# Retention's queries and keys computed with tokens on the partitions, in two blocks of 1024 columns

## The chip, the cores and the metric

One Trainium2 chip; the kernel runs on one of its cores. The metric is device microseconds from the start to the end of one execution, the median over several; lower is better. Four engines do the arithmetic: PE (TensorE, matrix multiply into PSUM), DVE (VectorE), ACT (ScalarE) and POOL (GpSimd, nearly unused here). SP (SyncE) issues most transfers. Each engine works through its own queue.

## The reference, cut to what matters

A decoder layer on 256 tokens of width 2048: a gated feed-forward half with its norm, two mixers side by side (retention and windowed attention), a second feed-forward half, and a gated embedding. All of it is float32. The change concerns how retention's queries and keys come out of the normalised stream `h`:

```python
rq, rk, rv, rg, aq, ak, av, gate_r, gate_a = jnp.split(h @ w_in[i], SPLIT_POINTS, axis=-1)
rq = rotary(rq.reshape(B, S, RET_HEADS, RET_DK), positions, RET_DK, RET_THETA)
rk = rotary(rk.reshape(B, S, RET_HEADS, RET_DK), positions, RET_DK, RET_THETA) * (RET_DK ** -0.5)
...
def rotary(x, pos, n_rot, theta):
    ...
    cos = jnp.cos(ang)[:, :, None, :]; sin = jnp.sin(ang)[:, :, None, :]
    x1, x2 = xr[..., :half], xr[..., half:]
    rot = jnp.concatenate([x1 * cos - x2 * sin, x2 * cos + x1 * sin], axis=-1)
```

Queries and keys are 1024 columns each (8 heads of 128); the product runs over 2048 rows of weights.

## The kernel before, in words

**Float32 by splitting.** Each float32 operand is split into a high part (a cast to the type `float32r`, on ACT) and a low part (operand minus high part, on DVE). A product is the sum of three matmuls: low by high, high by high, high by low. `ht` holds the normalised stream turned, with features on the partitions: for each of 16 blocks of 128 features, 256 tokens of the high part and 256 of the low part side by side.

**Two layouts of a product.** With *features on the partitions* (`features_out`, `features_chunk`, lines 461 and 469) the weights are the stationary operand: a high block meets all 512 columns of `ht` (high and low tokens at once), a low block only the 256 high ones. The result has features on the partitions; its two halves of 256 columns have to be added (`joined`, lines 1287 and 1288). With *tokens on the partitions* (`tokens_chunk`, `Sum.add`, lines 510 to 512) `ht` is the stationary operand and 512 columns of weights move, three matmuls a product.

**Chunks.** Weights come in chunks of 512 KB, a tile of 128 x 1024 float32. A `Single` unit is one chunk: one load, one cast on ACT (line 162) and one subtraction on DVE (line 164). In features layout a chunk takes 8 matmuls of 512 columns and 8 of 256, in tokens layout 12 of 512.

**Seven products for eight.** `block` computes two neighbouring groups of 512 columns with tokens on the partitions. A unit "P" is a pair of Singles (24 matmuls). A unit "S" (`Seven`) is one 2 x 2 step of Strassen's method in Winograd's form: 7 products, so 21 matmuls. It needs sums of the weights (`Seven.make`, lines 277 to 298: four passes on ACT, eight on DVE) and *forms* of the stationary operand (`forms_sums`, lines 588 to 591; `forms_split`), and at the end a common part (`seven_common`, lines 634 to 639) and four additions (lines 1669 to 1672).

**The order of the work.** Every engine's order is the program's. A planner emits it: `take` hands out the next unit that is made, and after its matmuls `done` frees its slots and calls `fill`, which makes units (the split) while less than 45 units of time lie ready, and loads further ones while less than 90 do. A Single counts 12, a Seven 21. `slots_for_weights(n)` says how many of the 46 slots of 4 KB per partition the planner may hold: a Single holds 1 loaded and 2 made, a Seven 2 loaded, 8 while it is made, 7 made. All other 4 KB tiles (sums, forms, rotated tables, results) take theirs from the same 46. PSUM has 8 banks, one per 512 columns of float32.

After each unit `run_side` runs one job of each of three lists: `side` (jobs in order), `slow` and `lazy` (generators that go on by one step). On `lazy` lies `sums_ahead`: in spare time it computes weight sums for the second feed-forward half and writes them to memory (lines 372 to 386).

**The stages around the change**, in `mixers`:
- *rv, first two column groups* (tokens layout, 16 Singles). The first six run while the norm before still turns its last rows (`norm.first`); the other ten run plainly, from about 713 us of the profile on, under `slots_for_weights(24)`. `values` then splits the four sums out of PSUM (lines 113 and 114).
- *rqk* (features layout): 8 groups of 256 columns, 4 chunks each, 32 in all, under `slots_for_weights(14)`. After each group `joined` writes a half tile. The generator `angles` on `slow` builds the table of cosines and sines (`rotary_table`, lines 993 to 1020) and then turns the groups (`turn_by_angle`, lines 1293 to 1297: a shuffle within the partitions and three passes).
- *rv, last two groups* (16 Singles), *rg* (retention's gate, 32 Singles) with retention itself on `side`, and then attention, the two mixing gates and the output projections. The gates `ga0` and `ga1` (1143 to 1226 us) and `mr0` and `mr1` (1269 to 1354 us) use Seven units. The forms of `ht` that the gates need are computed in the stage before them.

`Turn` turns a tile by a transfer: `part` separates the 16-bit words (two copies on ACT), `move` is a transposing DMA on SP's queue, `join` puts the words together (two copies on ACT).

Of the kernel before, what the change touches and what calls it, by code (L numbers as in the profile page):

```python
# [8 lines left out]
F32 = mybir.dt.float32  # L9
# [61 lines left out]
def layer(ctx: ExitStack, tc: tile.TileContext, io):  # L71
# [16 lines left out]
    def slot(shape, dt, name):  # L88
        return slots.tile(shape, dt, tag="slot", name=name)
# [1216 lines left out]
    RET_UNITS = [units_of(order, SEVEN[: order.count("S")]) for order in ("SPSPSPSP", "PSPSPPPP")]  # L1306
    gate_keys = lambda b: lambda n, p: ("w_in_f2", 29 + 4 * b + 2 * n, p)
# [33 lines left out]
    def mixers(ht, norm, residual, keepers, away):  # L1341
        rhs = lambda k: (ht[:, k, :S], ht[:, k, S:])
        both_halves = lambda k: ht[:, k, :]
        rq = [slot([P, 4, S], F32, f"rq{j}") for j in range(2)]
        rk = [slot([P, 4, S], F32, f"rk{j}") for j in range(2)]

        def rotated(grp, ps):
            who = (rq, rk)[grp // 4][grp % 4 // 2]
            to = who[:, grp % 2 * 2 : grp % 2 * 2 + 2, :]
            joined(ps, f"rr{grp}", to)  # L1350
            unturned[grp] = to

        unturned = {}

        def rotations():
            for grp in (0, 4, 1, 5, 2, 6, 3, 7):
                while grp not in unturned:
                    yield
                to = unturned.pop(grp)
                turn_by_angle(to, f"rr{grp}", to, *trig["r"], SH_R)  # L1360
                yield
                yield
# [29 lines left out]
        def angles():  # L1392
            yield from rotary_table("r")
            yield from rotations()
            yield from rotary_table("a")

        slow.append(angles())
# [240 lines left out]
        made = {}  # L1638
        forms = lambda p: made[p // 2](p % 2)
# [3 lines left out]
        for j in range(4):  # L1643
            def before(c, j=j):
                if j < 2:
                    return
                g = j - 2
                if c == 0:
                    sums = forms_sums(whole([ht[:, 4 * g : 4 * g + 4, :]], f"gaf{g}w"))
                    keep["f", g] = sums  # L1650
                if c == 1:
                    hi, lo = (slot([P, 8, P], F32R, f"gaf{g}{w}") for w in "hl")
                    made[g] = forms_split(keep.pop(("f", g)), hi, lo)
# [7 lines left out]

        def mixer_block(name, units, keys, lhs):

            ps = [banks(name + w) for w in "ab"]
            got = []
            block(name, units, keys, lhs, forms, block_sums(ps, units, KD), lambda *a: got.extend(seven_common(*a)))
            weave_all()
            e, w, z = got
            dve.tensor_tensor(e[:, 0], e[:, 0], ps[0][0], ALU.add)
            dve.tensor_tensor(e[:, 1], w[:, 1], ps[1][0], ALU.add)  # L1670
            for t in range(2):
                dve.tensor_tensor(z[:, t], z[:, t], ps[t][1], ALU.add)
            return [e, z]
# [400 lines left out]
```

## Time and profile before

| | |
|---|---|
| median of 3 runs | 2226.69 us (2225.88 to 2227.86) |
| profiled execution | 2229.62 us, of which its span on the core 2227.6 us |
| granted TensorE clock | 0.999 |
| PE busy | 2215.5 us (99%) |
| DVE busy | 2011.8 us (90%) |
| ACT busy | 1451.7 us (65%) |
| rqk's matmuls | first at 740.2 us, last at 829.4 us |

Times in the views are microseconds from the start of the span. In a timeline row the first number is the start, the second the busy time, then engine, line, operation, output<-input and count; square brackets give the idle time of the engine before and what ended it. A row with a count above 1 merges neighbours; starts that lie closer together than the busy time mean that the engine overlaps successive instructions.

### The profile page before, as it was taken

Reading aid. Unit: us, or ns where it says so; the run is one execution under the profiler, and the core shown is the slowest. Engines: PE = TensorE matmul, PEld = TensorE weight load, DVE = VectorE, ACT = ScalarE, POOL = GpSimd, SP = SyncE. Lnnn points to the kernel's source line nnn. Section 1 sums busy time; section 2 is a strip of 40 time slices with the busy share of each in tenths; the row PEclk is TensorE's granted clock in tenths of the full one; section 3 lists DMA queues with packets and bytes.
Section 4 is the critical chain, followed back from the end, with each engine's and each line's share of the span. In section 5 each row is a group of like instructions: output and inputs, shape, how many; then the busy total and the mean of one; then the engine's idle time right before and its main releaser. Section 6 shows DMA issues by size and latency. Waiting matters only on the chain.

```text
span 2227.6 us, 29127 instructions
## 1 busy us (share of the span) xinstructions
PE 2215.5 (99%) x10116; PEld 1832.7 (82%) x10116; DVE 2011.8 (90%) x2656; ACT 1451.7 (65%) x1691; POOL 48.4 (2%) x62
## 2 busy tenths in 40 slices
PE   9999999999999999999999999999999999999998
PEld 7788888888888888888788888888888877888887
DVE  5999999999988889889999888779999999899887
ACT  5877777777565545557866567466767678665553
POOL 0000000000000000000000000000000000000000
PEclk9999999999999999999999999999999999999999
DMA  9979889977686889846976578888899898777771
GB/s 315 259 227 264 249 241 263 255 239 235 225 301 238 296 280 331 274 171 228 293 232 232 174 216 323 306 302 269 290 313 312 292 265 260 215 242 234 283 290 69
DMA packets 303339, 573.91 MB, mean 258 GB/s; under 512 B 98764, under 2 KB 103756, under 8 KB 303192
## 3 DMA queue, kind: packets, MB, share of 16 engines
q1 hardware_dynamic: 293576, 541.70, 72.5%
q0 software_dynamic: 7632, 27.79, 6.7%
q10 hardware_dynamic: 1984, 2.58, 0.4%
q8 instruction: 79, 1.29, 0.2%
q14 instruction: 68, 0.56, 0.1%
HBM read 490.20 MB, written 33.55 MB: 235 GB/s over the span
## 4 chain that ended last, share of the span: by engine, by line
PE 92%; DMA 3%; DVE 3%; issue 2%; ACT 1%; SPq 0%; ACTq 0%; POOLq 0%; DVEq 0%
PE rqk L461 3%; PE f1g L512 3%; PE f1g L510 3%; PE f1g L511 3%; PE f2g L510 2%; PE f2g L511 2%; PE f2g L512 2%; PE f1u L512 2%; PE f1u L510 2%; PE f1u L511 2%; PE f2u L512 2%; PE f2u L510 2%; PE f2u L511 2%; PE aqk L461 2%; PE f2d L512 1%
## 5 line engine op out<-in xcount | busy, mean ns | idle before, releaser
L164 DVE TENSOR_TENSOR lw_in_f<-rw_in_f,hw_in_f 128x1024 fp32r<-128x1024 f32 x132 | 158.2, 1219 | 14.5 <-ACT hw_in_f L162 14.3
L164 DVE TENSOR_TENSOR lf_gu<-rf_gu,hf_gu 128x1024 fp32r<-128x1024 f32 x123 | 145.1, 1219 | 22.8 <-ACT hf_gu L162 22.1
L162 ACT CAST hf_gu<-rf_gu 128x1024 fp32r<-128x1024 f32 x123 | 123.3, 1048 | 29.7 <-DMA rf_gu<-in_f_gu 27.8
L293 ACT CAST hvf_gu<-vf_gu 128x1024 fp32r<-128x1024 f32 x83 | 87.5, 1055 | 76.5 <-DVE vf_gu L289 62.6
L284 ACT CAST huf_gu<-uf_gu 128x1024 fp32r<-128x1024 f32 x83 | 87.3, 1052 | 76.6 <-DVE uf_gu L280 69.3
L162 ACT CAST hw_in_f<-rw_in_f 128x1024 fp32r<-128x1024 f32 x132 | 132.5, 1049 | 6.9 <-DMA rw_in_f<-in_w_in_f 4.2
L164 DVE TENSOR_TENSOR lf_down<-rf_down,hf_down 128x1024 fp32r<-128x1024 f32 x96 | 115.6, 1220 | 20.5 <-ACT hf_down L162 16.3
L162 ACT CAST hf_down<-rf_down 128x1024 fp32r<-128x1024 f32 x96 | 98.5, 1049 | 27.3 <-DMA rf_down<-in_f_down 11.8
L287 DVE TENSOR_TENSOR lf_gu<-rf_gu,hf_gu 128x1024 fp32r<-128x1024 f32 x83 | 101.1, 1218 | 0.0
L298 DVE TENSOR_TENSOR lvf_gu<-vf_gu,hvf_gu 128x1024 fp32r<-128x1024 f32 x83 | 101.1, 1218 | 0.0
L296 DVE TENSOR_TENSOR luf_gu<-uf_gu,huf_gu 128x1024 fp32r<-128x1024 f32 x83 | 101.1, 1218 | 0.0
L277 ACT CAST hf_gu<-rf_gu 128x1024 fp32r<-128x1024 f32 x83 | 86.8, 1046 | 8.4 <-DMA rf_gu<-in_f_gu 8.4
L512 PE MATMUL f1g<-lf_gu,xt 128*128 128x512 f32 x223 | 87.1, 391 | 1.1 <-DVE lf_gu L164 1.1
L510 PE MATMUL f1g<-hf_gu,xt 128*128 128x512 f32 x223 | 87.0, 390 | 0.1
L511 PE MATMUL f1g<-hf_gu,xt 128*128 128x512 f32 x223 | 86.8, 389 | 0.0
L510 PE MATMUL f2g<-hf_gu,ht 128*128 128x512 f32 x196 | 76.4, 390 | 0.0
L512 PE MATMUL f2g<-lf_gu,ht 128*128 128x512 f32 x196 | 76.3, 389 | 0.0
L511 PE MATMUL f2g<-hf_gu,ht 128*128 128x512 f32 x196 | 76.3, 389 | 0.0
L512 PE MATMUL f1u<-lf_gu,xt 128*128 128x512 f32 x180 | 70.1, 390 | 0.0
L510 PE MATMUL f1u<-hf_gu,xt 128*128 128x512 f32 x180 | 70.1, 390 | 0.0
L511 PE MATMUL f1u<-hf_gu,xt 128*128 128x512 f32 x180 | 70.0, 389 | 0.0
L182 POOL DMA_DIRECT2D lf_gu<-rf_gu x37 | 32.2, 871 | 1636.9 <-DMA rf_gu<-in_f_gu 1105.6
(1568 smaller groups left out, 7220.3 us busy)
## 6 DMA issues: line engine op xcount, KB each, us to landing
rf_gu<-in_f_gu SPq DMA_DIRECT2D x362, 512.0 KB
rf_down<-in_f_down SPq DMA_DIRECT2D x176, 512.0 KB
rw_in_f<-in_w_in_f SPq DMA_DIRECT2D x148, 512.0 KB
lf_gu<-rf_gu POOLq DMA_DIRECT2D x37, 512.0 KB, 8.5
rw_rv<-in_w_rv SPq DMA_DIRECT2D x32, 512.0 KB
rw_ret<-in_w_ret SPq DMA_DIRECT2D x32, 512.0 KB
rw_mix<-in_w_mix SPq DMA_DIRECT2D x32, 512.0 KB
rw_pg<-in_w_pg SPq DMA_DIRECT2D x32, 512.0 KB
```

The costliest lines, as they stand in the source:

```text
L162: act.copy(c.hi, c.raw)
L164: dve.tensor_tensor(c.lo, c.raw, c.hi, ALU.subtract)
L277: act.copy(a.hi, a.raw)
L284: act.copy(uh, u)
L287: dve.tensor_tensor(a.lo, a.raw, a.hi, ALU.subtract)
L293: act.copy(vh, v)
L296: dve.tensor_tensor(ul, u, uh, ALU.subtract)
L298: dve.tensor_tensor(vl, v, vh, ALU.subtract)
L461: pe.matmul(ps[f], hi[:, kk, f * P : (f + 1) * P], rhs(k), start=k == 0, stop=k == n_k - 1,)
L510: pe.matmul(o, al, bh, start=first, stop=False)
L511: pe.matmul(o, ah, bh, start=False, stop=False)
L512: pe.matmul(o, ah, bl, start=False, stop=self.left == 0)
```

## The change

The eight feature groups of rqk become two calls of `mixer_block`, one for the queries (1024 columns) and one for the keys, with tokens on the partitions. Each is six P units and two S units: 14 units of the planner in place of 16 chunks. The order is PPPSPSPP and PPSPSPPP.

- The forms of `ht` for the four S positions (pairs 0 to 3) are built in the rv stage, at its units p = 4 and 5 (`forms_step`). They are dropped after the keys and built again for the gates as before.
- `rotary_table("r")` moves from rqk into the ten plain units of rv. At the eleventh step, after the first unit of the queries, `wide_tables` turns cosine and sine with four transposes on PE into one PSUM bank and spreads them with four copies on ACT to two tiles of 128 x 2 x 512.
- Each block gives two result tiles with tokens on the partitions. `rotated` turns each by the angle (two crossed products of 512 columns with runs of 16, one product and one addition of 1024) and then by a transfer: `part`, `move`, `join`. The queries' 13 side jobs run beside the keys' units, the keys' beside the third group of rv.
- `joined`, the shuffles and `turn_by_angle` no longer run for retention. The table for attention (`rotary_table("a")`) starts when the keys are joined.
- `sums_ahead` runs 2 items with 3 units between steps and then 5 with 2, in place of 3 and 4 with 2.

```diff
+    QK_UNITS = [units_of(order, SEVEN[: order.count("S")]) for order in ("PPPSPSPP", "PPSPSPPP")]
+    qk_keys = lambda b: lambda n, p: ("w_in_f2", 4 * b + 2 * n, p)
...
-        for grp in range(8):
-            plan_features([("w_in_f", grp)], KD)
+        for b in range(2):
+            block_units(QK_UNITS[b], qk_keys(b))
...
+        def forms_step(g, step):
+            if step == 0:
+                sums_of[g] = forms_sums(whole([ht[:, 4 * g : 4 * g + 4, :]], f"gaf{g}w"))
+            else:
+                hi, lo = (slot([P, 8, P], F32R, f"gaf{g}{w}") for w in "hl")
+                made[g] = forms_split(sums_of.pop(g), hi, lo)
...
+        def wide_tables():
+            cos, sin = trig["r"]
+            ps = bank("rtab").rearrange("p (w t n) -> p w t n", w=2, t=2)
+            for j, v in enumerate((cos, sin)):
+                for t in range(2):
+                    pe.transpose(ps[:, j, t], v[:, t * P : t * P + P], ident)
+            for j, w in enumerate("cs"):
+                wide[w] = slot([P, 2, 512], F32, f"rtab{w}")
+                for t in range(2):
+                    act.copy(
+                        wide[w][:, t].rearrange("p (h n) -> p h n", h=4), ps[:, j, t][:, None, :].broadcast_to([P, 4, P])
+                    )
+
+        def rotated(v, name, to):
+            halves = lambda x: x.rearrange("p t (q two n) -> p two (t q) n", two=2, n=16)
+            crossed = {}
+            def cross():
+                x = crossed["x"] = slot([P, 2, 512], F32, name + "x")
+                for two in range(2):
+                    dve.tensor_tensor(
+                        halves(x)[:, two], halves(v)[:, 1 - two], halves(wide["s"])[:, two], ALU.mult
+                    )
+            def scale():
+                dve.tensor_tensor(v, v, wide["c"], ALU.mult)
+            def add():
+                dve.tensor_tensor(v, v, crossed.pop("x"), ALU.add)
+                crossed["t"] = Turn(v, name)
+            def join():
+                to.append(slot([P, 4, S], F32, name + "t"))
+                crossed.pop("t").join(to[-1])
+            return [
+                cross, scale, add, lambda: crossed["t"].part(), lambda: crossed["t"].move(), idle, join,
+            ]
...
         slots_for_weights(24)
+        def angles():
+            yield from rotary_table("r")
+            wide_tables()
+            yield
+            while len(rk) < 2:
+                yield
+            yield from rotary_table("a")
+        slow.append(angles())
         for p in range(FRONT_PAIRS, KD // 2):
             for n in range(2):
+                if p in (4, 5):
+                    forms_step(p - 4, n)
                 u = take(("w_rv", n, p))
...
         slots_for_weights(14)
-        lazy.append(sums_ahead(ahead[:3], 3, 2))
-        lazy.append(sums_ahead(ahead[3:7], 2, 2))
-        for grp in range(8):
-            ps = banks(f"rqk{grp}")
-            features_out([(("w_in_f", grp), ps)], KD, both_halves)
-            rotated(grp, ps)
+        lazy.append(sums_ahead(ahead[:2], 3, 3))
+        lazy.append(sums_ahead(ahead[2:7], 2, 2))
+        for b in range(2):
+            got = mixer_block("rqk"[0] + "qk"[b], QK_UNITS[b], qk_keys(b), rhs)
+            jobs = [rotated(v, f"r{'qk'[b]}{n}", (rq, rk)[b]) for n, v in enumerate(got)]
+            side.extend(jobs[0][:3] + [jobs[0][3], jobs[1][0], jobs[0][4], jobs[1][1], jobs[1][2], jobs[1][3], jobs[1][4], jobs[0][6], idle, jobs[1][6]])
+        made.clear()
```

`mixer_block` itself only moves up in the file, and `forms_step` takes over the two steps that the gates' stage had written out.

More of the change, by code (lines that the diff above doesn't have):

```diff
@@ L1343, in mixers @@
         both_halves = lambda k: ht[:, k, :]
[L1344 to L1362, printed above, removed]
+        rq, rk = [], []
@@ L1636, in mixers @@
             attention_features(grp)
-        made = {}
-        forms = lambda p: made[p // 2](p % 2)
         lazy.append(sums_ahead(ahead[7:10], 2, 2))
@@ L1646, in before @@
                     return
[L1647 to L1653, printed above, removed]
+                if c < 2:
+                    forms_step(j - 2, c)
             ps = banks(f"gt{j}")
@@ L1660, in mixers @@
         assert not side
[L1662 to L1673, printed above, removed]
         slots_for_weights(22)
```

22 lines of the change are left out of this document (17 added, 5 removed).

## The prediction

> **What bounds the kernel now.** I read the page first, then the busy times by stage, then rqk's own instructions, then DVE's queue around the start of rqk, because several parts of the change land there.
>
> ```profile
> span 2227.6 us, 29127 instructions
> PE 2215.5 (99%) x10116; PEld 1832.7 (82%) x10116; DVE 2011.8 (90%) x2656; ACT 1451.7 (65%) x1691; POOL 48.4 (2%) x62
> DVE  5999999999988889889999888779999999899887
> PE 92%; DMA 3%; DVE 3%; issue 2%; ACT 1%; SPq 0%; ACTq 0%; POOLq 0%; DVEq 0%
> 717.00:740.20 23.20, 23.20 (x104) 19.23 (x103) 13.66 (x13) 14.01 (x16) 0.00 (x0) 1.00 1.02 396
> 740.20:785.00 44.80, 44.80 (x258) 39.41 (x258) 39.40 (x60) 22.67 (x31) 0.00 (x0) 1.00 0.77 265
> 829.70:873.10 43.40, 43.40 (x193) 35.95 (x192) 42.74 (x63) 22.41 (x27) 0.00 (x0) 1.00 0.98 344
> 1143.40:1226.00 82.60, 82.60 (x370) 68.19 (x370) 80.88 (x98) 51.43 (x57) 0.00 (x0) 1.00 0.63 214
> ```
>
> PE carries the chain. In the stage rows (window, length, then busy time of PE, weight loads, DVE, ACT) PE is busy for the whole of each window, so a microsecond of matmuls removed is a microsecond gained, and a microsecond of idle PE is one lost. DVE is the second engine: 13.66 of 23.20 us before rqk, 39.40 of 44.80 in its first half, 42.74 of 43.40 just behind it. The gates' stage, with eight Seven units, runs at 80.88 of 82.60 and PE still isn't idle. So a full DVE is bearable as long as it works far enough ahead.
>
> **The matmuls.** First timeline and chain rows, then the group that shows PE's only wait in the blocks of this kind.
>
> ```profile
> 735.25 0.39 PE L512 MATMUL rv<-lw_rv,ht 128*128 128x512 f32 x1
> 737.29 0.39 PE L512 MATMUL rv<-lw_rv,ht 128*128 128x512 f32 x1
> 740.01 0.39 PE L512 MATMUL rv<-lw_rv,ht 128*128 128x512 f32 x1
> 740.24 1.98 PE L461 MATMUL rqk<-ht,hw_in_f 128*128 128x512 f32 x8
> 742.21 0.95 PE rqk L469 x8
> 743.16 1.84 PE rqk L461 x8
> L512 PE MATMUL mr1a<-lw_ret,rett 128*128 128x512 f32 x26 | 10.2, 393 | 0.5 <-DVE lw_ret L164 0.5
> ```
>
> A chunk in tokens layout: twelve matmuls lie between 737.29 and 740.01, so 2.72 us, 0.227 each. A chunk in features layout: 0.95 + 1.84 = 2.79 us. rqk before is 32 x 2.79 = 89.3 us. After, 24 Singles take 65.3 and 4 Sevens of 21 matmuls 4 x 4.76 = 19.0 us, together 84.3. Gain 5.0 us: 2.2 from the shape, 2.8 from the twelve matmuls that are gone. The rows bind this term to a few tenths.
>
> [...] Here eight matmuls of 256 columns took 0.95 us, 0.119 each, more than half of 0.227; the trace decides.
>
> **What is moved ahead of the queries.** rv's ten plain units now share DVE with the forms and the first table. These rows are DVE's queue there now, and the prices of what joins it.
>
> ```profile
> 712.08 9.17 DVE L164 TENSOR_TENSOR lw_rv<-rw_rv,hw_rv 128x1024 fp32r<-128x1024 f32 x8 [3.07 <-ACT hw_rv L162]
> 723.78 1.23 DVE L114 TENSOR_TENSOR ht<-lnr,ht 128x1024 fp32r<-128x1024 f32 x1 [2.52 <-ACT ht L113]
> 724.92 2.35 DVE L164 TENSOR_TENSOR lw_rv<-rw_rv,hw_rv 128x1024 fp32r<-128x1024 f32 x2
> 727.19 4.62 DVE L164 TENSOR_TENSOR lw_in_f<-rw_in_f,hw_in_f 128x1024 fp32r<-128x1024 f32 x4
> 737.66 1.37 DVE L114 TENSOR_TENSOR rvl<-rv,rvh 128x512 fp32r<-128x512 f32 x2 [5.84 <-ACT rvh L113]
> 740.52 0.33 ACTq L990 DMA_DIRECT2D pos_ir<-in_positions  x1
> 744.29 0.28 DVE L993 CAST posr<-pos_ir 128x256 f32<-128x256 int32 x1
> 746.72 1.22 DVE L164 TENSOR_TENSOR lw_in_f<-rw_in_f,hw_in_f 128x1024 fp32r<-128x1024 f32 x1
> 747.86 0.88 DVE L1006 SCALAR_TENSOR_TENSOR rotr<-rotr 128x256 f32<-128x256 f32 x2
> 758.86 0.28 DVE L1010 TENSOR_SCALAR rotr<-rotr 128x256 f32<-128x256 f32 x1
> 765.30 0.35 DVE L1014 TENSOR_SCALAR trigr<-rotr,cst 128x256 f32<-128x256 f32 x1
> 766.89 1.22 DVE L164 TENSOR_TENSOR lw_in_f<-rw_in_f,hw_in_f 128x1024 fp32r<-128x1024 f32 x1
> 1095.75 1.22 DVE L612 TENSOR_TENSOR gaf0w<-ht 128x1024 f32<-128x1024 f32 x1
> 1098.47 1.22 DVE L164 TENSOR_TENSOR lw_in_f<-rw_in_f,hw_in_f 128x1024 fp32r<-128x1024 f32 x1
> L113 ACT CAST f1forms<-sums x4: 1049/1052/1056, 470.9 to 505.9; 128x1024 fp32r<-128x1024 f32 x4
> ```
>
> Number the rv units 0 to 15. Eight low parts from 712.08 on are those of units 6 to 13; the two at 724.92 are 14 and 15. They are made early: PE reaches the low part of unit 14 at 735.25 (its third matmul, counted back from 740.24). DVE is then idle for 5.84 us, waiting for PE. In program order the change puts in front of unit 14's low part (made after unit 10, when fewer than 45 units of time are ready): the table's second step, 744.29 to 746.72, 2.43 us; the sums of the first forms, 1095.75 to 1098.47, 2.72; a pair of the table, 0.88; the forms' low part, which waits for ACT's cast of 1.05; a second pair; the second sums, 2.72. From 724.92: 727.35, 730.07, 730.95, (cast until 731.12) 732.27, 733.15, 735.87, and the low part of unit 14 ends 1.22 later at **737.09, 1.84 us late**. (Spacing of consecutive passes of 1024: 9.17 / 8 = 1.15.) Behind it: the third pair 737.90, the second forms' low part 739.05, unit 15's low part 740.27; PE, by then late, wants it at 737.09 + 2.72 = 739.81. Ten matmuls follow: rv ends at 742.54, **2.30 us later**. The table's load of positions comes from ACT's queue, 0.33 us of issue one unit ahead of its first pass; it had landed before 744.29 from an issue at 740.52, so DVE doesn't wait for it. With 712 to 735 as given, half a microsecond either way in the order of these passes is all I can see, so 1.3 to 3.3.
>
> **The table's transposes.** After the queries' first unit PE itself transposes the table, in its queue, so everything behind waits too. They need the cosine and a PSUM bank. Of 8 banks the queries' sums hold four; the other four were rv's sums, or, if the queries took those, the queries wait themselves. So DVE must have split a sum of rv first. DVE's queue from 739.05 goes on: unit 15 740.20, the last of the seven table terms 0.4, the next Single 741.75, the clamp (758.86) 0.28, two Singles 744.33, the table's end 765.30 to 766.89, 1.59, 745.92, one Single 747.07, first split of rv:
>
> ```profile
> L113 ACT CAST rvh<-rv x8: 589/589/589, 737.0 to 873.3; 128x512 fp32r<-128x512 f32 x8
> L114 DVE TENSOR_TENSOR rvl<-rv,rvh x8: 679/692/692, 737.7 to 874.0; 128x512 fp32r<-128x512 f32 x8
> L1020 ACT ACTIVATE trigr<-rotr x1: 417/417/417, 767.0 to 767.0; 128x256 f32<-128x256 f32 x1
> 701.74 0.60 PE L780 MATMUL lnps<-ident,f1y 128*128 128x128 f32 x4
> ```
>
> ACT's cosine ends at 746.34, its cast of the sum at 746.93, DVE's split at 747.76. PE is there at 742.54 + 2.72 = 745.26 and waits **2.50 us**, then four transposes, **0.60**. If another bank were free, only the cosine would hold it: 1.08. The other end, with DVE a microsecond later: 3.5. I take 2.5.
>
> **Within the two blocks.** DVE per part, before and after:
>
> ```profile
> L1288 DVE TENSOR_TENSOR rq<-rqk,rr0lo x2: 417/418/418, 751.8 to 752.1; 128x256 f32<-128x256 f32 x2
> L1293 DVE STREAM_SHUFFLE rr0sh<-rq x1: 736/736/736, 770.3 to 770.3; 128x512 f32<-128x512 f32 x1
> L1295 DVE TENSOR_TENSOR rq<-rq,trigr x4: 692/693/693, 771.1 to 829.5; 128x512 f32<-128x512 f32 x4
> 1146.91 0.69 DVE L279 TENSOR_TENSOR uw_in_f<-rw_in_f 128x512 f32<-128x512 f32 x1
> 1153.33 0.69 DVE L279 TENSOR_TENSOR uw_in_f<-rw_in_f 128x512 f32<-128x512 f32 x1
> ```
>
> Removed: eight groups of 2 x 0.42 + 0.74 + 3 x 0.69 = 3.65, 29.2 us, and eight Singles' low parts, 9.8. Added: four Sevens of 6.42 (1146.91 to 1153.33), 25.7; two common parts of 6 x 0.69 + 1.22, 10.7; four rotations of 2 x 0.69 + 2 x 1.22 = 3.8, 15.3. No row shows a product with runs of 16; it lies between L1295's 0.69 and the shuffle's 0.74, and I take 0.69. Net 12.7 us more, of which half of the rotations and the last four additions, 10.4, fall behind the keys. In the queries' block DVE needs about 12 x 1.15 + 2 x 6.42 + 2.6 + 5 for a first item of weight sums = 34 us of PE's 42; it catches up after the transposes. In the keys' block it has some 12 x 1.15 + 12.8 + 2.7 + 2.6 + 7.6 + 5 = 44.5 of 42; rv behind starts with DVE about 3 us less ahead, which the lead of three Singles, 8.2 us, covers.
>
> The one tight place is the second Seven of each block. With 14 slots the first one holds 7, so the second (2 + 6) is loaded and made only when the first is done, two Singles, 5.4 us, ahead of its use, with 6.42 of DVE behind the load. What hides it: the 46 slots together have a good dozen idle there by my count of the living tiles, so SP and DVE run ahead of that point. Bounds: 0, as in the gates' stage, to the price of the rival below; I take 0.5, the one wait in the projection's blocks (0.5, lw_ret). The four turns cost ACT two copies and a join each and SP a transposing issue; ACT has half its time free (22.67 of 44.80), and the loads queued behind SP's issue are for units some 20 us ahead. Hidden: 0. The moved sums for the second half run 12 units longer, into rg. Nothing waits for them there: 0.
>
> **The sum.** -5.0 + 2.3 + 2.5 + 0.6 + 0.5 = **+0.9 us**, on the profiled execution's 2229.62 (span 2227.6 and 2.0 around it), which lies 2.9 above the median of 2226.69. On the median: **2227.6**.
>
> **Rivals.** *Faster.* DVE catches up before it matters, for instance because passes overlap more than I allow, and PE loses only the transposes: -5.0 + 0.6 = -4.4, 2222.3. For it: DVE idles 9.5 of the 23.2 us before rqk. Against it: 5.84 of those are one wait at the end, behind unit 15's low part, and the queue above is counted pass by pass. [...]
>
> *Slower.* The second Sevens come late. If the idle slots give no head start, the load of two chunks begins with the 5.4 us: 1.05 MB at 396 GB/s, the most a row shows, 2.6 us, then 6.42, so 3.6 us late, twice: +0.9 - 0.5 + 7.2 = +7.6, 2234.3. It decides from 2.1 us late each on. Against it: the engines run ahead of PE here (the low parts of the first four rqk chunks, 727.19 + 4.62, were done 8 us before use).
>
> *The early waits are double.* Forms and table each delay by 2 more us (ACT's casts queue behind each other): +4.9, 2231.6. Part of the range, at the edge of a change that can be told.
>
> **Chances.** About 0.2%, 4.5 us, is what a measurement of this kernel can tell from no change. The forecast 0.62; the faster rival 0.20, half of it beyond 4.5 us, since its price lies on that edge; late second Sevens 0.10; double early waits 0.08, half of it beyond 4.5 us. So faster 0.10, the same 0.76, slower 0.14. The range 2222.0 to 2233.0 reaches to the faster rival's price and past the double waits, and leaves out about 1 in 10 on either side.
>
> **What would show it.** rqk's blocks have 372 matmuls at 0.227 us; PE waits for `lw_rv` near 735 to 740 and once more before four transposes of the table, near 745; the keys end about where they end now, near 830. No wait of PE for `lu` or `lv` of a Seven above 1 us. I am wrong if PE goes through rv and the table without waiting, or if the second Sevens hold it.

## The result and the profile after

The changed kernel takes 2234.66 us in the median (2233.63 to 2238.66), the kernel before 2226.64 (2225.88 to 2227.86): ratio 1.004, 95% interval 1.0027 to 1.0053. It is **8.0 us slower**; 0.9 us was predicted. The profiled execution of after took 2234.48 us, near its median; that of before lay 3 us above its own, so the two spans differ by only 5.0.

First the page of after, then its list of PE's waits (total, times, longest, in us).

```profile
span 2232.6 us, 28924 instructions
...
PE 2213.7 (99%) x9980; PEld 1827.5 (82%) x9980; DVE 2032.5 (91%) x2666; ACT 1475.6 (66%) x1707; POOL 48.4 (2%) x62
...
PE 89%; DVE 4%; DMA 4%; ACT 2%; issue 1%; SPq 0%; ACTq 0%; POOL 0%; DVEq 0%; POOLq 0%
```

```profile
PE ro L1501 <- DVE rsp L114: 6.0, 2, 5.2
PE rv L512 <- DVE lw_rv L164: 1.9, 1, 1.9
...
PE rtab L1378 <- ACT trigr L1020: 1.1, 1, 1.1
```

PE has 136 matmuls fewer and is busy 1.8 us less, yet the span is longer. The last two waits are the two that the prediction had in its sum. The first isn't: `ro` is retention's product of scores and values, in rg, behind everything that the change touches.

By stage, after (queries and keys; rv's third and fourth group; rg), then before (queries and keys; rg). Columns: window, length, busy time of PE, weight loads, DVE, ACT, POOL; granted clock, DMA share, GB/s.

```profile
739.84:826.14 86.30, 85.22 (x377) 70.05 (x376) 82.61 (x98) 56.88 (x65) 0.00 (x0) 1.00 0.73 237
826.14:869.66 43.52, 43.52 (x193) 36.04 (x192) 34.48 (x39) 27.20 (x28) 0.00 (x0) 1.00 1.04 345
869.66:976.70 107.04, 101.02 (x463) 84.24 (x462) 95.80 (x200) 60.07 (x75) 0.00 (x0) 0.97 0.85 294
```

```profile
740.24:829.61 89.37, 89.37 (x513) 78.67 (x512) 79.39 (x118) 42.30 (x57) 0.00 (x0) 1.00 0.79 270
873.14:970.86 97.72, 97.72 (x463) 82.15 (x462) 80.29 (x170) 56.41 (x69) 0.00 (x0) 1.00 0.74 245
```

From the same matmul of rv (712.90 before, 709.92 after) the stages sum up: rv's end +2.6 (27.34 to 29.92), queries and keys -3.1, rv's last groups 0.0, **rg +9.3**. The rest is no effect of the change that I can name: after is 3.0 earlier before that matmul and 0.8 shorter behind rg. -3.0 + 8.8 - 0.8 = 5.0, the difference of the spans. So up to rg the change costs nothing (2.6 - 3.1 + 0.0), and rg loses everything. In rv's last groups PE is full in both, but DVE is busy 34.48 of 43.52 us, where the prediction's row of before has 42.74 of 43.40: it stands idle there with DMA at a share of 1.04.

PE in rg, after (timeline; the count merges neighbours), and the stage behind the wait:

```profile
878.95 0.39 PE L512 MATMUL rg<-lw_in_f,ht 128*128 128x512 f32 x1
884.54 0.80 PE L1501 MATMUL ro<-rvh,rsp 128*128 128x256 f32 x2 [5.20 <-DVE rsp L114]
...
887.05 0.63 PE L511 MATMUL rg<-hw_in_f,ht 128*128 128x512 f32 x1
887.48 0.63 PE L512 MATMUL rg<-lw_in_f,ht 128*128 128x512 f32 x1
...
890.77 0.40 PE L511 MATMUL rg<-hw_in_f,ht 128*128 128x512 f32 x1
```

```profile
884.54:890.54 6.00, 6.00 (x19) 5.13 (x20) 5.93 (x14) 3.74 (x6) 0.00 (x0) 0.50 1.02 400
```

The wait is 5.20 us, and it costs more than itself: for 6 us behind it the granted clock is 0.50 ("half clock" below), and the matmuls start 0.43 apart in place of 0.227. That is 3.0 us more. With 0.8 for the second wait (near 957) these make 9.0 of the 9.3.

Where the wait comes from stands in the chain of waits, read up to that matmul:

```profile
856.25 8.27 DMA mrk<-wrk
...
864.73 5.88 DMA pos_ia<-in_positions
...
870.63 0.30 DVE posa L993
...
879.29 1.13 DVE lw_in_f L164
880.42 0.33 DVE rsc L1480
...
882.79 1.22 DVE lw_in_f L164
884.01 0.48 DVE rsp L114
...
884.54 2.29 PE ro L1501 x9
```

The keys' transposing transfer, then the positions' load (issued from ACT's queue behind the join that waits for that transfer), then the first pass of attention's table, and from there DVE without a pause until `rsp`. DVE's and ACT's own rows of that stretch, after; then DVE's before:

```profile
841.29 0.69 DVE L372 TENSOR_TENSOR uf_gu<-rf_gu,rf_gu 128x512 f32<-128x512 f32 x1 [4.19 <-DMA rf_gu<-in_f_gu]
...
862.69 1.22 DVE L164 TENSOR_TENSOR lw_in_f<-rw_in_f,hw_in_f 128x1024 fp32r<-128x1024 f32 x1
...
864.62 1.36 ACT L238 COPY rk1t<-mrk 128x1024 uint16<-128x1024 uint16 x1 [2.15 <-DMA mrk<-wrk]
...
869.07 1.23 DVE L164 TENSOR_TENSOR lw_in_f<-rw_in_f,hw_in_f 128x1024 fp32r<-128x1024 f32 x1 [3.83 <-ACT hw_in_f L162]
...
873.01 1.22 DVE L164 TENSOR_TENSOR lw_in_f<-rw_in_f,hw_in_f 128x1024 fp32r<-128x1024 f32 x1
...
876.07 1.22 DVE L164 TENSOR_TENSOR lw_in_f<-rw_in_f,hw_in_f 128x1024 fp32r<-128x1024 f32 x1
877.21 0.88 DVE L1006 SCALAR_TENSOR_TENSOR rota<-rota 128x256 f32<-128x256 f32 x2
...
880.87 0.87 DVE L1006 SCALAR_TENSOR_TENSOR rota<-rota 128x256 f32<-128x256 f32 x2
```

```profile
866.20 1.22 DVE L164 TENSOR_TENSOR lw_in_f<-rw_in_f,hw_in_f 128x1024 fp32r<-128x1024 f32 x1
...
868.47 2.35 DVE L164 TENSOR_TENSOR lw_in_f<-rw_in_f,hw_in_f 128x1024 fp32r<-128x1024 f32 x2
...
871.94 1.22 DVE L164 TENSOR_TENSOR lw_in_f<-rw_in_f,hw_in_f 128x1024 fp32r<-128x1024 f32 x1
...
876.72 0.42 DVE L1424 TENSOR_TENSOR rsc<-rs,dec 128x256 f32<-128x256 f32 x1 [0.58 <-PE rs L1421]
```

These rows give a measure that the prediction lacked, DVE's **lead**: from the end of a chunk's low part to the third matmul of the chunk, PE's first use of it. rg's chunks are 2.72 us apart, so chunk 0 is due at 869.66 + 0.45, chunk 3 at 878.27. After: 870.11 - 863.91 = 6.2, then 2.5, 1.3 and 1.0. Before, with rg at 873.14: 6.2, 6.6, 8.2, 8.6. The scores stand in the same queue right behind chunk 3, and no pass between can be skipped. From chunk 3's low part (877.29) to `rsp` ready (884.48) DVE works for 7.2 us without a pause; PE wants `rsp` at 879.34, 1.1 after it wants chunk 3. So a lead of 6.1 at chunk 3 is needed, 1.0 was there, and PE waits for the difference. Before, 8.6 were there.

### The profile page after: what moved, and what is told of

Same layout as the page of the kernel before. It is cut to its first block, busy times and chain, and to the rows that moved or that the text cites. A ratio compares the mean times of both kernels' runs of the same rounds, so it can differ in the third digit from the quotient of the medians.

```text
span 2232.6 us, 28924 instructions
## 1 busy us (share of the span) xinstructions
PE 2213.7 (99%) x9980; PEld 1827.5 (82%) x9980; DVE 2032.5 (91%) x2666; ACT 1475.6 (66%) x1707; POOL 48.4 (2%) x62
## 4 chain that ended last, share of the span: by engine, by line
PE 89%; DVE 4%; DMA 4%; ACT 2%; issue 1%; SPq 0%; ACTq 0%; POOL 0%; DVEq 0%; POOLq 0%
PE f2g L512 2%; PE f2g L511 2%; PE f2g L510 2%; PE f1g L510 2%; PE f1g L512 2%; PE f1g L511 2%; PE f2u L512 2%; PE f1u L512 2%; PE f1u L510 2%; PE f1u L511 2%; PE f2u L511 2%; PE f2u L510 2%; PE aqk L461 2%; DMA rf_gu<-in_f_gu 2%; PE f2d L512 1%; PE f1e L511 1%
## 5 line engine op out<-in xcount | busy, mean ns | idle before, releaser
L164 DVE TENSOR_TENSOR lw_in_f<-rw_in_f,hw_in_f 128x1024 fp32r<-128x1024 f32 x124 | 148.7, 1219 | 17.3 <-ACT hw_in_f L162 17.2
L293 ACT CAST hvf_gu<-vf_gu 128x1024 fp32r<-128x1024 f32 x83 | 87.5, 1054 | 76.2 <-DVE vf_gu L289 64.7
L162 ACT CAST hw_in_f<-rw_in_f 128x1024 fp32r<-128x1024 f32 x124 | 125.4, 1048 | 6.1 <-DMA rw_in_f<-in_w_in_f 3.9
L298 DVE TENSOR_TENSOR lvf_gu<-vf_gu,hvf_gu 128x1024 fp32r<-128x1024 f32 x83 | 101.4, 1222 | 0.0
L296 DVE TENSOR_TENSOR luf_gu<-uf_gu,huf_gu 128x1024 fp32r<-128x1024 f32 x83 | 101.4, 1221 | 0.0
L287 DVE TENSOR_TENSOR lf_gu<-rf_gu,hf_gu 128x1024 fp32r<-128x1024 f32 x83 | 101.4, 1221 | 0.0
```

The lines of the kernel that those rows point to most:

```text
L162: act.copy(c.hi, c.raw)
L164: dve.tensor_tensor(c.lo, c.raw, c.hi, ALU.subtract)
L287: dve.tensor_tensor(a.lo, a.raw, a.hi, ALU.subtract)
L293: act.copy(vh, v)
L296: dve.tensor_tensor(ul, u, uh, ALU.subtract)
L298: dve.tensor_tensor(vl, v, vh, ALU.subtract)
```

## The experiments

Theories: **A**, attention's table in rg is in front of `rsp`; **B** and **E**, the keys' turn (ACT's join, or the transfer's hold on DMA and SP) makes weights late; **C**, the moved weight sums; **D**, too much DVE work from forms and Sevens. Ratios are against the kernel before, with 95% intervals; "first wait" is PE's wait for `rsp` near 880 (5.2 after the change), "second wait" the one near 950 (0.8).

**One part at a time.** Edits to the changed kernel:

```diff
 a_early:    -            while len(rk) < 2:
             -                yield
 sums_late:  +            while len(gate_v) < 1:      # ahead of sums_ahead(ahead[2:7], 2, 2)
             +                yield
 one_form:   -                if p in (4, 5):
             +                if p == 4:
 plain:      -("PPPSPSPP", "PPSPSPPP")
             +("PPPPPPPP", "PPPPPPPP")                # and no forms_step
```

> Attention's rotary table no longer waits for the keys' turn; its eleven steps follow retention's table and run beside the queries' block, so none of its passes is left in rg. Theory A (about 6 us of DVE for this table, in the middle of retention's first scores, made rsp late): PE's 5.2 us wait for rsp and the 6 us at half clock behind it go, rg takes 98 to 99 us in place of 107.0, the time is 2226 to 2228 us. Theory B (the keys' transposing transfers and their joins on ACT hold DVE up ahead of rg): the join stays where it is, so a wait for rsp of 3 us or more stays, 2232 to 2235. Theory C (the weight sums for the second half, which now run into rg, delay rsp): as B, 2232 to 2235.

2237.56, ratio 1.005 (1.0037 to 1.0064). The first wait is still 3.0. Beside the blocks the table costs PE 3.5 us (waits of 1.2, 1.0 and 1.3 us for low parts), so DVE enters rv's last groups later and the lead at chunk 3 is 1.6. A alone isn't the cause, and the blocks have no room for the table. Two of the three waits in the blocks are for a Seven's low parts (1.2 and 1.3).

> The last five items of weight sums for the second half start only when the first pair of groups of rg is done; all else is as after the change. Theory C (their passes are what makes rsp late): the wait for rsp goes, rg takes 98 to 99 us, 2226 to 2228. Theory A (attention's table makes it late): two passes of sums, 2.4 us, leave the queue ahead of rsp, the wait falls from 5.2 to between 2.8 and 4, and the clock drop may stay: 2230 to 2234. Theory B (the turn): DVE's idle time ahead of rg stays, 2232 to 2235.

2232.38, ratio 1.0027 (1.0017 to 1.0037). The first wait is gone, and rg takes 98.7 us. The rows show why: chunk 0 and 1 are ready 5 and 8 us earlier, and the table, not delayed either, starts 7 us ahead of rg.

```profile
857.90 1.22 DVE L164 TENSOR_TENSOR lw_in_f<-rw_in_f,hw_in_f 128x1024 fp32r<-128x1024 f32 x1
...
861.08 1.23 DVE L164 TENSOR_TENSOR lw_in_f<-rw_in_f,hw_in_f 128x1024 fp32r<-128x1024 f32 x1 [1.96 <-ACT hw_in_f L162]
862.36 0.29 DVE L993 CAST posa<-pos_ia 128x256 f32<-128x256 int32 x1
```

The gain in rg, 8.3, doesn't reach the end: held back as a whole, the sums run into attention, where PE waits 2.6 us for a rotated query and runs 3.4 us at half clock behind that.

> The forms of pairs 2 and 3 aren't built in rv: the queries' and keys' Sevens use pairs 0 and 1 alone, and the gates build all four again. Nothing else changes. If the early wait comes from the two forms in DVE's queue: PE's wait of 1.94 us for lw_rv goes to below 0.3, and with rg as it is the time is 2232 to 2233. Theory D (DVE simply has too much to do up to rg, whatever the work): about 4 us less DVE work and two slots more reach rg too, the wait for rsp falls by some 3 us and 2227 to 2230 comes out.

2233.69, ratio 1.0027 (1.0016 to 1.0038). Each block has two S units, and both blocks use pairs 0 and 1 for them, not four positions as the section on the change has it; so the second set of forms has no reader before the gates build it anew. Without it both early waits are gone (the table's transposes don't wait either), and rg starts 3.9 us earlier, counted from the same matmul of rv. But the leads are 6.2, 2.6, 1.2, 0.9 and the first wait 5.3, and the second wait grows to 2.7 with a half clock of its own, 3.4 us at 0.50: rg takes 110 us. Most of the early gain is given back (rg takes 3.0 more than after the change); D in this form falls.

> Both blocks are eight plain pairs: no Sevens, no forms in rv; two copies of 512 columns out of PSUM in place of the four additions and the common part; the rotation, its table, the turn and attention's table stand where the change put them. The layout alone: 32 chunks at 2.72, 87.3 us of matmuls, 2.8 more than with Sevens, and no wait of 1.94 us in rv. Theory A or B (attention's table or the turn makes rsp late, not the amount of DVE work): rg's loss of 9 us stays, 2234.7 + 2.8 - 1.9 = 2235.6, 2234 to 2237. Theory D (too much DVE work from forms and Sevens): rg's loss goes, 2226 to 2228.

2229.71, ratio 1.0012 (1.0003 to 1.0021). No first wait, with the turn and the table in place. DVE enters rv's last groups with a lead of 13.6 us in place of 5.3, and 6.3 are left at chunk 3. So how far DVE is ahead when the keys end decides as much as what delays it afterwards: the Sevens' DVE work is part of the cause, though PE doesn't wait for it in the blocks. The time stays above D's 2226 to 2228; a second wait of 1.8 us is left in rg.

**Which delay.**

```diff
 no_move:   +            if self.name.startswith("rk"):   # move(): the join reads the words as they lie
 a_mid:     -            while len(rk) < 2:
            +            while len(rq) < 2:
 dec_late:  one decay table loaded at the keys' end, the others one by one ahead of two_heads(h + 2)
 best1:     one_form, a_mid and dec_late together
```

> The transposing transfer of the keys is left out (the join reads the words as they lie, so the keys' tiles hold untransposed data); attention's table, forms, Sevens and the join's copies on ACT stay as after the change. Theory E (the transfers keep all 16 DMA engines busy at 1.0 to 1.1 of their share from 820 to 890 and hold SP's queue for 6 to 8 us each, so weights come late and DVE stands idle 8 us ahead of rg): the two idle times of DVE of about 4 us go, rg takes 98 to 100 us in place of 107.0, the time is 2226 to 2228. Theory A (attention's table in rg is enough by itself): the table still stands in front of rsp, the wait stays at 3 us or more, 2231 to 2235.

2234.22, ratio 1.0032 (1.0019 to 1.0044). DVE's stop of 3.8 us shrinks to 1.6, that of 4.2 stays (4.0). The first wait is 2.4, the second 2.8. Of the wait, half of what E expected; of the time, nothing: rg still takes 106.6 us, since behind each of the two waits the granted clock is 0.50 for 3.4 us. The keys of this kernel stay untransposed, so it serves to measure and not to use.

> Attention's table starts when the queries are joined, so that its passes run beside the third group of rv, where DVE was idle for 9 of 43.6 us, and not beside the queries' block or in rg. Theory A (the table's passes in rg, 6 us of DVE, are needed for the loss): with them gone and the two blocks not disturbed, the wait for rsp falls from 5.2 to 0 to 2, the half clock goes, 2227 to 2229. Theory E (weights late because of DMA): the passes fall into idle time, but the lateness of casts and low parts stays: a wait of 2 to 4 us, 2231 to 2234.

2231.75, ratio 1.0022 (1.0013 to 1.0031). First wait 1.3, without half clock; second 2.6, with 3.4 us at 0.50 behind it. The first wait is as A has it, the time as E has it.

> Three of the four decay tables (384 KB each) are loaded within rg, each ahead of its two heads, in place of all four at the start of rv's third group: 1.2 MB, about 3 us at 396 GB/s, leave the stretch where the DMA engines are full, and three slots stay free. Theory E (DMA): the lateness ahead of rg shrinks by up to 3 us, the wait for rsp from 5.2 to 2 to 3, 2229 to 2232. Theory A or D (DVE's work): no change, 2233 to 2236.

2234.06, ratio 1.0032 (1.0020 to 1.0043). First wait 3.7, leads 8.4, 4.8, 2.9, 2.5: 1.5 us of lead from taking away 3 us of DMA (an estimate of the expectation). E's direction, about half its size, and no gain in the time that could be told: the second wait has grown from 0.8 to 2.4.

> One set of forms, attention's table beside rv's third group, and decay tables loaded within rg, together. If A and E are both part of the cause and one set of forms removes the early waits: rv's end 2.5 us earlier than after the change, no wait of 1 us for the table, rg 98 to 100 us, 2222 to 2226 in all. If the cause lies elsewhere: rg stays above 104 us, 2230 to 2234.

2227.38, ratio 1.0004 (0.9995 to 1.0013). First wait 0.3, rv's end 2.6 earlier, no wait for the table. rg takes 103, for the second wait is 2.8, with 3.4 us at half clock; so 98 to 100 and 2222 to 2226 were missed. Why the second wait grows, from 0.8 after the change to between 2.4 and 2.8 in five of these variants, no run shows directly; best7 below removes what is left of it.

**The sums' tail, and the table in the kernel before.** In `sums_tail` and `best2` the seventh item moves to the gates' stage; `plain_best` is best2 with plain pairs; `before_a_late` delays the table in the kernel before.

```diff
 sums_tail:      -sums_ahead(ahead[2:7], 2, 2)   ...  -sums_ahead(ahead[7:10], 2, 2)
                 +sums_ahead(ahead[2:6], 2, 2)   ...  +sums_ahead(ahead[6:10], 2, 2)
 before_a_late:  +            while len(rv) < 3:
                 +                yield
                 +            for _ in range(5):
                 +                yield
```

> The seventh item of weight sums for the second half is moved out of rg to the gates' stage (four items in place of five at two units' distance, the later list starts one item earlier); all else is as after the change. The moved-sums theory C: these items now end eight steps, about 25 us, earlier, near where they ended before the change, so the second wait (near 957, 0.8 us after the change, 2.4 to 2.8 in four of the variants) goes; the first wait of 5.2 us near 884 has the same passes ahead of it and stays: rg 105 to 107 us, 2232.5 to 2234.5. If the second wait comes from retention's own passes: no change, 2234 to 2236.

2234.76, ratio 1.0040 (1.0028 to 1.0053). No gain: waits of 6.0 and 1.5. Without the tail both waits are longer, not shorter; C as stated here falls.

> One set of forms, attention's table beside rv's third group, decay tables loaded in rg, and the seventh item of weight sums moved to the gates' stage. That version without the last edit took 2227.4 us and had one large wait left in rg, 2.8 us near 950 with 3 us at half clock behind it. If the moved sums cause it: no wait above 1 us in rg, rg 98 to 99.5 us, 2222 to 2224.5. If retention's own passes cause it: 2227 to 2228.5.

2224.17, ratio 0.9993 (0.9984 to 1.0002). One wait is left, 1.8 near 946, with 3.4 us at half clock behind it. The edit that gained nothing in sums_tail takes the second wait from 2.8 to 1.8 here, and rg from 102.9 to 101.4: half of what was expected.

> The same with eight plain pairs in both blocks, no Sevens and no forms. If the prediction's two terms for the matmuls are right (2.2 us from the layout, 2.8 from the twelve matmuls of four Sevens) and no wait is left in either version, this is 2.8 us above the version with Sevens and 1.6 below the kernel before, 2225 to 2226. If the Sevens' DVE work still costs PE something elsewhere, it is nearer than 2 us to that version.

2226.20, ratio 0.9999 (0.9990 to 1.0008), no wait in rg. It takes 2.0 us more than best2, and 3.4 more than best7 below, where no wait is left either: around the predicted 2.8. The two blocks by themselves take 87.5 us here and 85.0 in best7, 2.6 more.

> The kernel before the change with one edit: attention's table waits until rv's third group is split and five units more, so its passes run in rg at the place where the change put them. In the kernel before, the first rsp was ready 2.4 us ahead of its matmul and DVE had 0.8 us of idle time ahead of the first scores. Theory A (5 to 6 us of table passes ahead of rsp are enough): a wait of 2 to 3 us for rsp, perhaps with some us at half clock, 2229 to 2232. Theory E (it takes weights late from the transposing transfers, so that DVE is behind already): no wait above 1 us, 2226 to 2228.

2226.99, ratio 1.0002 (0.9993 to 1.0011). No wait. The test is weaker than meant: with no join in its way the positions landed early, and the table began 7.4 us ahead of rg, not 1.0 behind its start.

```profile
859.68 2.35 DVE L164 TENSOR_TENSOR lw_in_f<-rw_in_f,hw_in_f 128x1024 fp32r<-128x1024 f32 x2
...
862.95 0.29 DVE L993 CAST posa<-pos_ia 128x256 f32<-128x256 int32 x1 [0.91 <-DMA pos_ia<-in_positions]
```

With a lead of 11 to 14 us the passes that do fall into rg cost nothing.

**The load or the join, and the version without them.** `sums_before` gives the weight sums the spacing of before the change. `join_late` puts three idle jobs ahead of the keys' last join and keeps the table's start in place. `best5` is best2 with that join; `best6` is best5 with the old spacing in place of the moved seventh item.

> The weight sums for the second half run at the spacing that they had before the change (3 items at two units' distance, then 4). DVE's lead is the time from the end of a chunk's low part to PE's use of it: 6.2 to 8.6 us for the first four chunks of rg before the change, 6.2, 2.5, 1.3, 0.9 after it. If the new spacing decides (DVE stood idle 4.2 us near 841 for a load of these sums): that idle time goes, the lead at the third chunk is 4 us or more, the first wait for rsp is below 2, 2228 to 2231. If the keys' join on ACT decides: the lead still falls by 3 us or more at the second chunk, the wait stays above 4, 2233 to 2236.

2241.95, ratio 1.0067 (1.0055 to 1.0080), the worst of all. The prediction's slower rival appears after all, in the keys' block alone, together with a first wait of 7.3. Rows of the list of PE's waits, then DVE's first pass for the keys' second Seven:

```profile
PE ro L1501 <- DVE rsp L114: 7.3, 1, 7.3
...
PE rks L512 <- DVE lw_in_f L287: 2.1, 1, 2.1
PE rks L512 <- DVE luw_in_f L296: 1.4, 1, 1.4
```

```profile
804.40 0.69 DVE L279 TENSOR_TENSOR uw_in_f<-rw_in_f 128x512 f32<-128x512 f32 x1 [3.05 <-DMA rw_in_f<-in_w_in_f]
```

DVE stands for a load, and SP's queue shows why it is late. At the old spacing an item's low part comes behind the keys' first Seven on DVE (795.59). SP stores it at 796.83, issues nothing between 782.46 and then, and issues the next loads of weights only behind it (797.26). After the change SP issues five loads in that time (781.61 to 795.94). So the spacing that the change brings is needed where it is; neither expectation holds.

> The last join of the keys comes three units later, so that ACT doesn't stand in front of it while the transposing transfer runs; the transfers and attention's table stay where they were. If the join on ACT decides: DVE's idle time of 3.8 us near 869 goes, the lead of the second to fourth chunk of rg is 4 us or more in place of 2.5 to 0.9, the first wait is below 2.5 in place of 5.2, 2228 to 2231. If the transfer itself decides (it takes the DMA engines and SP's queue from the loads): the loads are as late, the lead stays below 3, 2233 to 2236.

2235.47, ratio 1.0035 (1.0022 to 1.0048), waits 4.3 and 2.8. DVE's stop near 869 is gone and the lead of chunk 1 is 6.0, but chunk 3 is at 3.1 again, because ACT now stands in front of a load, issued behind the transposing transfer:

```profile
870.51 1.05 ACT L162 CAST hw_in_f<-rw_in_f 128x1024 fp32r<-128x1024 f32 x1 [3.52 <-DMA rw_in_f<-in_w_in_f]
```

(SP issued that load at 865.58, behind the 6.61 us that the transposing transfer held its queue.) DVE's one stop of 3.8 us comes back as three of 0.2, 1.4 and 0.9, the last of them between chunk 3 and `rsp`, and 7.4 of lead are needed here. B's gain doesn't come. Neither expectation holds as written; the loads are late as E has it, the lead of chunks 1 and 2 is what B has.

> One set of forms, attention's table beside rv's third group, decay tables in rg, the seventh item of sums moved, and the keys' last join three units later. Without the last edit 2224.2 us, with leads of 4.2, 2.7, 4.3, 4.7 us at the first chunks of rg and a wait of 1.8 near 945. If the join still costs lead there: leads of 4 to 6; the wait near 945 comes from retention's own join and stays, so 2223.5 to 2225. If PE's idle time near 945 depends on the lead carried through rg: it goes too, 2221.5 to 2223.5.

2226.13, ratio 0.9999 (0.9990 to 1.0008): a first wait of 1.1 comes back, and 1.8 near 949 stays. Chunk 3's lead is 5.5, but with the join put off 6.6 are needed.

> The same, but with the weight sums at the spacing of before the change in place of the moved seventh item. If the sums' spacing decides, at least as good: 2221.5 to 2224. If their DVE passes in the queries' block hold the Sevens: waits for lu or lv of 1 us or more, 2224 to 2227.

2231.76, ratio 1.0020 (1.0011 to 1.0030): PE waits 2.2 and 1.4 for a Seven of the keys. That is the wait of the second expectation, but in the other block, and the time lies 4.8 us above its range.

> Two of the parts taken away together: attention's table runs beside rv's third group, and the transposing transfer of the keys is left out (the keys' tiles hold untransposed data). Alone, the first took PE's first wait for rsp from 5.2 to 1.3 us, the second to 2.4. If the parts feed one backlog of DVE and add up: no first wait, a lead of 4 us or more at the first chunks of rg, 2229 to 2231 with the early waits and the one near 957 still there. If one of them masks the other: a wait of 1 us or more stays.

2227.57, ratio 1.0005 (0.9997 to 1.0014). First wait 0.3, lead at chunk 3 4.3, second wait 1.2, no half clock in rg. Two parts that alone leave 1.3 and 2.4 leave 0.3 together. They help together, but don't add up in full: alone they bring the lead at chunk 3 from 1.0 to 3.2 and to 3.8, which would add to 6.0.

> The version that took 2224.2 us (one set of forms, attention's table beside rv's third group, decay tables in rg, the seventh item of sums moved), with the join of retention's second turned half one unit later. There ACT stood 2.5 us in that join and DVE 4.1 us behind it ahead of the scores near 944. If that stop causes the last wait of 1.8 us: it goes, 2221.5 to 2223.5. If the wait comes from loads that are late: it stays, 2223.5 to 2225.

The edit is one more `idle` ahead of `ret3b(1)`. **2222.82, ratio 0.9982 (0.9973 to 0.9991)**: 3.6 us faster than the kernel before, and 12 us below the change as it was. No wait in rg above 0.3 us, though DVE still stops 3.1 us there; by stage (blocks, rv's last groups, rg):

```profile
738.23:823.19 84.96, 84.96 (x377) 70.17 (x376) 81.55 (x97) 55.74 (x65) 0.00 (x0) 1.00 0.73 239
823.19:867.69 44.50, 44.09 (x193) 35.91 (x192) 40.57 (x59) 27.35 (x30) 0.00 (x0) 1.00 0.98 323
867.69:966.06 98.37, 98.06 (x463) 82.04 (x462) 85.78 (x175) 57.16 (x70) 0.00 (x0) 1.00 0.88 302
```

**What the runs say together.** Lead of chunk 3 in rg, first wait, and their sum, in us:

| kernel | lead | first wait | sum |
|---|---|---|---|
| after | 1.0 | 5.2 | 6.2 |
| one_form | 0.9 | 5.3 | 6.2 |
| sums_tail | 0.2 | 6.0 | 6.2 |
| sums_before | -1.1 | 7.3 | 6.2 |
| dec_late | 2.5 | 3.7 | 6.2 |
| no_move | 3.8 | 2.4 | 6.2 |
| plain | 6.3 | 0.1 | |
| sums_late | 10.3 | 0 | |
| a_early (no table in rg) | 1.6 | 3.0 | 4.6 |
| a_mid (no table in rg) | 3.2 | 1.3 | 4.6 |
| no_move_a, best7 (no table in rg) | 4.3 | 0.3 | 4.6 |

The sums are of unrounded figures. As long as DVE doesn't stop, a sum is the DVE work between chunk 3 and `rsp`, less the 1.1 us by which PE wants `rsp` later: 6.2 us of lead are needed with the table's passes there, 4.6 without. The difference of 1.6 is the two pairs of the table's passes in the rows of after, 0.79 each from start to start. (With the join put off it changes: join_late needs 7.4.) So the constant sum says that what lies in between stayed the same; what took the lead is read from the first column. Every part that shortened the first wait did it by the lead or by the work in between. Holding back the sums, or leaving out the Sevens, is enough by itself; moving the table or leaving out the transfer is not. So no part is the cause by itself: they draw on one stock.

## Why the prediction was wrong, point by point

*The step that failed* is the sentence on the work behind the keys: "rv behind starts with DVE about 3 us less ahead, which the lead of three Singles, 8.2 us, covers." Its first half was on the safe side: at the first chunk of rv's third group DVE is 5.3 us ahead after the change and 6.3 before. "Covers" failed. From there to chunk 3 of rg the lead falls to 1.0, where before has 8.6 and 6.2 are needed. It was counted on for the Sevens and then for the work behind the keys, which was put at nothing:
- The turns, "Hidden: 0". ACT's free time was the wrong resource. SP's queue is held 6.30 us by the transfer of the keys' second turn, the next load of weights is issued behind it at 862.65, and ACT stands 2.15 us in its queue until the transfer lands; the low part made next stood 3.8 us for its cast. Without the transfer the lead at chunk 3 is 2.8 larger.
- The weight sums, "Nothing waits for them there: 0". DVE itself waits for them, in order: 4.2 us near 841 for their load. With the last five items held back the lead is 9.3 larger, and rg 8.3 shorter. This is the price of doing these sums here at all, not of moving them: before starts three items between the end of the keys and the first `rsp`, at 831.4, 853.5 and 870.7, and has the lead for it; after starts two, at 841.3 and 859.9. No run shows a cost of the new spacing: with the old one the lead is 2.1 smaller.
- Attention's table, which the same wait moves from rv's last groups into rg, was not costed: 1.6 us between chunk 3 and `rsp`, and 2.3 of lead (a_mid).
- The Sevens' work on DVE was allowed for, with 3 us, but as covered. With plain pairs the lead at chunk 3 is 5.3 larger.

These are not shares that add up to the loss, as no_move_a shows.

None of these was visible as a wait of PE before; the needed lead, 6.2, and what each part takes of it are what the prediction should have set against the 8.6 there. And a half clock behind a long wait, 3.0 us, was in no term.

*The terms that held.* rv's end was put 2.3 late: PE waited 1.94 for the low part of unit 14 (worked out: 1.84), and the stage lost 2.6. DVE's passes came in the order that was worked out. The matmuls, 84.3: the blocks without waits took 86.30 - 1.08 - 0.66 = 84.6, in best7 84.96 with the transposes in; against 89.37 before that is a gain of 4.8, where 5.0 was put. The second Sevens were on time (0.5 allowed, 0 measured).

*A term that was mis-sized.* The table's transposes waited 1.08, not 2.5: only the cosine held them, the case given as a lower end, so a PSUM bank was free: PE ran them at 743.80, and DVE split the first sum of rv at 744.35. This wait and that of 1.94 vanish without the second set of forms (one_form). That nothing reads this set in these blocks could have been seen in the code.

*The rivals.* The faster one didn't occur. The slower one gave a time near the truth, 2234.3, by a mechanism that wasn't there: that is luck. Waits for a Seven's low parts appeared in variants alone: 2.1 + 1.4 us and 2.2 + 1.4 with the old spacing of the sums, 1.2 and 1.3 with the table beside the blocks.

## What to carry to other kernels

When an in-order engine serves both a stock of prepared weights and a short chain that another engine waits for, measure its lead in front of that chain, in microseconds, and charge every new pass, stop and moved job against that one number: costs that are each hidden draw on the same stock. Follow moved work to where it lands, through the queue that issues its loads, before calling it free. Look also for work that nobody reads. And look behind a gain: dropping that work alone made rg begin 3.9 us earlier here, and rg took 3.0 longer.

## What was not expected of the hardware

- **Behind short waits of PE its granted clock was 0.50, for 3.4 us or two or three times that.** Stretches at 0.50 lasted 3.4 us behind waits of 1.8 to 3.0 (eighteen of them), 6.8 at 3.7 to 6.0 (five), 10.2 at 7.3 (one); part of the longer ones lies within the wait (0.7 of 6.8 after the change). Added up from stage rows of 1 us they are 3.42 (no_move), 6.82 (after) and 10.24 (sums_before). Why they have these lengths no run shows. (The last 3 to 7 us of every run, 4.7 before and 3.9 after, are at 0.50 as well and aren't counted.) All waits of 2.57 us and more brought one, none below 1.78 by itself; between them it went either way: 1.78 (best2) and 2.40 (no_move) did it, 1.81 (plain), 2.00 (best6) and 2.43 (dec_late) didn't. The wait for rv's unit 14, 1.94 to 1.96 us in ten kernels, did it in six (dec_late, join_late, no_move, no_move_a, sums_before, sums_tail) and not in four (after, a_early, a_mid, sums_late), so the length doesn't decide there. (It cost nothing there: in dec_late rv is 1.3 us longer than after the change, and the blocks, without the wait for the cosine, are 1.3 shorter.) So a first wait cut from 5.20 to 2.40 (no_move) kept 3.4 us at 0.50 behind it, and one of 2.43 (dec_late) had none. Stage rows of best2, where `ro` starts at 946.86 behind its wait of 1.78:

```profile
945.86:946.86 1.00, 0.00 (x1) 0.00 (x1) 1.00 (x3) 0.60 (x1) 0.00 (x0) 1.00 1.05 417
946.86:947.86 1.00, 1.00 (x6) 1.00 (x7) 1.00 (x3) 0.49 (x2) 0.00 (x0) 0.66 1.01 406
947.86:948.86 1.00, 1.00 (x6) 1.00 (x6) 1.00 (x2) 1.00 (x3) 0.00 (x0) 0.50 1.02 410
...
949.86:950.86 1.00, 1.00 (x4) 0.77 (x4) 0.96 (x3) 1.00 (x2) 0.00 (x0) 0.64 1.06 418
950.86:951.86 1.00, 1.00 (x6) 0.81 (x5) 0.90 (x5) 0.82 (x1) 0.00 (x0) 1.00 0.92 365
```

- **The keys' transposing transfers, beside full DMA engines, held SP's queue for 8.22 and 6.30 us, the queries' for 3.03 and 1.82.** The keys' second half of 512 KB took 8.27 us from issue to landing, while the DMA engines' share was 1.08 and the rate fell to 266 GB/s (860 to 870), against 399 at a share of 1.02 from 830 to 839, ahead of the first turn. Behind the queries' issues, at 799 and 816, the share was 0.85 and 0.87 (8 us each). 0.52 MB in 8.27 us is 63 GB/s, beside other loads.
